# Hybrid encoder trunk: eight weight pieces of the second layer's gated MLP are cast, and their residuals formed, by transfers of GpSimd's queue

## The chip, the cores and the metric

The kernel runs on one core of one Trainium2 chip. The metric is the device time of one execution in microseconds (us). Before the change it is 857.34 us, the median of three runs (857.09 to 857.48).

The engines are TensorE (PE, matrix products; PEld is its loading of weights), VectorE (DVE), ScalarE (ACT), GpSimd (POOL) and SyncE (SP). SP issues nearly all transfers from DRAM. The matrix product reads its operands from on-chip memory and sums in PSUM.

## The reference

Two layers work on 256 tokens of width 1024. Each has a token mixer (pooling and dilated attention) and a gated MLP with a width-3 convolution. The change concerns the MLP's first product in the second layer:

```python
def _conv_ffn(xn, w_up, conv_w, conv_b, w_down):
    a, gval = jnp.split(xn @ w_up, 2, axis=-1)      # w_up: 1024 x 5632 (two halves of 2816)
    ...
    return (jax.nn.gelu(a) * gval) @ w_down

for layer in range(DEPTH):                          # DEPTH = 2
    h = h + _token_mixer(_rmsnorm(h, norm1[layer]), ...)
    h = h + _conv_ffn(_rmsnorm(h, norm2[layer]), w_up[layer], ...)
return _rmsnorm(h, norm_f)
```

All is float32. The weights are read once each, so the kernel streams them past 256 tokens.

## The kernel before

**Products in three passes.** The PE multiplies in the format float32r (fp32r in the profile). To keep float32 accuracy, each operand is split into a high part (the value cast to fp32r) and a low part (the value minus the high part). A product is then high x high + high x low + low x high, all summed in PSUM. For activations the parts lie in one tile (`x2`); for weights they are `wh` and `wl`.

**The class `Weights` (object `W`)** streams the weights. A *load* is a transfer of mostly 1 MB from DRAM into one of three `raw` buffers (`RAW`), issued by SP (L126). A *piece* is half a load, 128 x 1024 elements. Splitting a piece (`open_next`) is two instructions: ACT casts `raw` to `wh` (L191), then DVE subtracts `wh` from `raw` into `wl` (L192). There are five buffers for such pairs (`BUFS`). `get` hands the next piece to the products and first splits pieces ahead of it, in the MLP up to four ahead; `free` gives its buffers back after the products. So the cast of a piece waits until the PE has finished an older one.

**The order in the MLP.** `ORDER` lists the blocks: a0 g0, a1 g1, ... a4 g4, r5 are blocks of 512 columns of `w_up` (a and g are its two halves, r5 is the rest of both), and d0 to d4 are parts of `w_down`. A block has 1024 rows x 512 columns, that is four pieces of 256 rows; `by_rows` (L671) gets a piece, calls `v_sum` (L661) for both halves of the tokens, six products each, so twelve products of 128x512 a piece, and frees it. After a block DVE turns the sums by 32x32 blocks, SP moves the turned blocks between partitions (`up_turned<-up_rows`, 64 KB each, L691), and `two_up` (L1384) works out the convolution and the gate on ACT and DVE, alongside the products of later blocks.

The block a0 is begun inside the norm before it: `residual_mm` (L567) ends the mixer's output product, `Norm.add` (L456) adds up the squares of the new rows, POOL adds the parts (L467, L469) and takes the root (L472, `rstd`), DVE scales the rows (L485, `xn`), and the PE transposes them (L494, `xt_ps`). While this goes on for the second half of the tokens, the PE has 18 products of a0 on the first half to do (`begin_mlp`, L1318).

`keep_order` (L643) fixes the order of PE, ACT and DVE to that of the program text in this part. POOL and SP are ordered by the scheduler.

The tile `m2` (16 KB a partition) holds the merged branches of the mixer; its last readers are the output product's matmuls. In the second layer it is not used after that.

Of the kernel before, what the change touches and what calls it, by code (L numbers as in the profile page):

```python
# [10 lines left out]
F32 = mybir.dt.float32  # L11
F32R = mybir.dt.float32r
AF = mybir.ActivationFunctionType
ALU = mybir.AluOpType
AX = mybir.AxisListType

P = 128
D = 1024
# [8 lines left out]
DFF = 2816  # L27
# [10 lines left out]
PAIRS = (0, 1)  # L38
POOLED = {15: 0, 17: 1, 19: 2, 21: 3}
ORDER = "a0 g0 v0 a1 g1 a2 g2 a3 g3 a4 g4 r5 d0 d1 d2 d3 d4"  # L40
RING = 16
TWOS = (16, 20, 24, 28, 32, 36, 39, 43, 47, 51, 55)
VISITS = {
    "score": ((0, 1), (2, 3), (5, 6), (7, 8)), "expo": (3, 5, 8, 10), "norm": (4, 6, 9, 11),
    "turn": (5, 7, 10, 12), "parts": (13, 14, 19, 20), "weigh": (15, 16, 20, 21),
# [41 lines left out]
class Weights:  # L87
# [4 lines left out]


    RAW, BUFS, LOOK = 3, 5, 3

    def __init__(self, tc, pool, idle):
        self.tc, self.nc, self.pool, self.idle = tc, tc.nc, pool, idle
        self.loads, self.pieces = [], []
        self.n_loaded, self.n_split, self.n_got = 0, 0, 0
        self.raw, self.split = {}, {}  # L100
        self.live = set()
        self.behind, self.n_behind = (), 0
        self.n_scaled, self.gains = 0, None
        self.due = 0

    def add(self, src, shape, cuts, tag=None):

        n = len(self.loads)
        self.loads.append((src, shape, tag))
        return [(n, cut, c_shape) for cut, c_shape in cuts]  # L110

    def use(self, pieces, slots=()):
        slots = list(slots) + [None] * len(pieces)
# [35 lines left out]
    def _split(self, upto):  # L149
        nc = self.nc  # L150
        self.load(self.due)
        first = self.n_split
        while self.n_split < len(self.pieces):
            i = self.n_split
            n, cut, shape, slot = self.pieces[i]
            if i >= upto and (slot is None or i >= max(upto, first + 2) or i >= upto + 4 or i < 4):
                break
            if slot is None and len(self.live) == self.BUFS:
                break
            self.load(n + 1)  # L160
            with ExitStack() as queued:
                if i < self.n_behind:
                    for inst in self.behind:
                        queued.enter_context(self.tc.issue_after(inst.ins))
                for part in self.open_next():
                    for make in part:
                        make()
            self.due = n + self.RAW

    def open_next(self):  # L170

# [50 lines left out]
def encoder(ctx, tc, x, w_in, w_pool, pool_scale, w_a, w_b, w_o, norm1, norm2, w_up, conv_w,  # L222
# [11 lines left out]
    W = Weights(tc, wpool, big)  # L234
# [8 lines left out]
    def rows(w, r0, n=2, c0=0, width=1024, tag=None, pieces=2):  # L243

        src = w[r0 : r0 + n * P, c0 : c0 + width].rearrange("(k p) c -> p k c", p=P)
        h = n // pieces
        return W.add(
            src, (n, width), [((lambda t, j=j: t[:, j * h : (j + 1) * h, :]), (h, width)) for j in range(pieces)],
            tag,
        )  # L250

    for l in range(DEPTH):
        if l == 0:
            slots = (("m2", 0, 2), ("m2", 1, 2), ("ybig",), ("at2",))
            for j in range(2):
                kept = rows(w_in[l], j * 512, 4, C_V, 512)
                more = rows(w_in[l], j * 512, 4, C_V + 512, 512, "k1" if j else None)
                for n in range(2):
                    W.use(kept[n : n + 1], slots[2 * j + n : 2 * j + n + 1])
                    W.use(more[n : n + 1])  # L260
            W.n_scaled = len(W.pieces)
        else:
            W.use(rows(w_in[l], 512, 4, C_V, 512), (("ybig",), ("at2",)))
            for j in range(2):
                W.use(rows(w_in[l], j * 512, 4, C_V + 512, 512))

        def half_of(w, c0, half, n):
            for j in range(n):
                W.use(rows(w, j * 512, 4, c0 + half.start, 512))

        for half in HALVES:
            half_of(w_in[l], 0, half, 2)
        for c0 in (C_Q + 512, C_K + 512, C_Q + 1024, C_K + 1024):
            half_of(w_in[l], c0, HALVES[0], 2)
        for c in PAIRS:
            q = cols(w_in[l], C_Q + c * 256)
            k = cols(w_in[l], C_K + c * 256)
            if c == 0:
                pool = W.add(
                    w_pool[l].rearrange("g (k p) c -> p (g k) c", p=P), (8, 256),  # L280
                    [((lambda t, j=j: t[:, 4 * j : 4 * j + 4, :]), (4, 256)) for j in range(2)],
                )
                q.insert(1, pool[0])
                k.insert(1, pool[1])
            W.use(q + k)
        half_of(w_in[l], C_V + 1024, HALVES[0], 2)

        for half in HALVES:
            half_of(w_in[l], C_GP, half, 2)
        for half in HALVES:  # L290
            half_of(w_a[l], 0, half, 2)
            half_of(w_in[l], C_GA, half, 2)
            half_of(w_b[l], 0, half, 1)
        for c in range(4):
            W.use(rows(w_o[l], c * 256))
        slots = (("v1",), ("ybig",), ("at2",))
        for kind, n in ORDER.split():
            n = int(n)
            if kind == "v":
                if l + 1 < DEPTH:  # L300
                    W.use(rows(w_in[l + 1], 0, 4, C_V, 512), (("m2", 0, 2), ("m2", 1, 2)))
                continue
            for j in range(2):
                if kind == "d":
                    W.use(rows(w_down[l], (4 * n + 2 * j) * P))
                elif kind == "r":
                    src = w_up[l][j * 512 : (j + 1) * 512].rearrange("(k p) c -> p k c", p=P)
                    c0 = (4 * n * P, 4 * n * P + DFF)
                    W.use(
                        W.add(  # L310
                            tuple(src[:, :, c : c + 256] for c in c0), (4, 2, 256),
                            [
                                ((lambda t, j=j: t[:, 2 * j : 2 * j + 2].rearrange("p k h c -> p k (h c)")), (2, 512))
                                for j in (0, 1)
                            ],
                        )
                    )
                else:
                    p = rows(w_up[l], j * 512, 4, (kind == "g") * DFF + 4 * n * P, 512)
                    W.use(p, slots[2 * j : 2 * j + 2] if (kind, n) == ("a", 0) else ())  # L320
        W.use(rows(w_down[l], (NF - 2) * P))


    h = const.tile([P, 2, D], F32, name="h")
# [578 lines left out]
    for l in range(DEPTH):  # L903
# [296 lines left out]
        for c in PAIRS:  # L1200
            for n in range(4):
                src, rest = (halves(a) for a in proj(x2))
# [85 lines left out]
        m2 = []  # L1288
# [29 lines left out]
        def begin_mlp():  # L1318
# [12 lines left out]
            out=way[:, 0].rearrange("p j c r -> p c j r"),  # L1331
            in_=th[0][:, 1].rearrange("p (c j r) -> p c j r", c=4, j=4),
# [132 lines left out]
        for kind, n in ORDER.split():  # L1465
# [20 lines left out]
            n = int(n)  # L1486
# [39 lines left out]
```

## Time and profile before

| | |
|---|---|
| Device time, median of 3 runs | 857.34 us |
| Span of the profiled execution, first to last instruction | 856.1 us |
| Granted TensorE clock | 0.999 of full speed |
| POOL busy | 19.9 us, 53 instructions |
| DMA from DRAM | 160.65 MB read, 190 GB/s over the span |

The profile gives for its execution the span alone; the median of the timed runs lies 1.24 us above it, and what lies around the span (start and end of the program) is in that difference. The shares of busy time are means over stages; a stage is read from windows of the span. Matmuls are pipelined: one of 128x512 is shown as 0.39 us long, and the next starts before it ends, so a full PE is seen from the distance of the starts.

Two parts of the pipeline matter below. From about 669 us the PE does the second layer's a0; the blocks g0 to g4 run from 680.92 us. Twelve products make a piece. The pieces are numbered through the program: a0 has 230 to 233, g0 234 to 237, a1 238 to 241, and so on to g4 with 266 to 269.

### The profile page before, as it was taken

Reading aid. Unit: us, or ns where it says so; the run is one execution under the profiler, and the core shown is the slowest. Engines: PE = TensorE matmul, PEld = TensorE weight load, DVE = VectorE, ACT = ScalarE, POOL = GpSimd, SP = SyncE. Lnnn points to the kernel's source line nnn. Section 1 sums busy time; section 2 is a strip of 40 time slices with the busy share of each in tenths; the row PEclk is TensorE's granted clock in tenths of the full one; section 3 lists DMA queues with packets and bytes.
Section 4 is the critical chain, followed back from the end, with each engine's and each line's share of the span. In section 5 each row is a group of like instructions: output and inputs, shape, how many; then the busy total and the mean of one; then the engine's idle time right before and its main releaser. Section 6 shows DMA issues by size and latency. Waiting matters only on the chain.

```text
span 856.1 us, 11279 instructions
## 1 busy us (share of the span) xinstructions
PE 849.1 (99%) x4030; PEld 713.0 (83%) x4030; DVE 648.8 (76%) x918; ACT 476.9 (56%) x700; POOL 19.9 (2%) x53
## 2 busy tenths in 40 slices
PE   9999999999999999999999999999999999999997
PEld 7888888888888888888888889888888888888886
DVE  6967898566767788999656597986568658999874
ACT  7735475444545566767444445654445436766762
POOL 1120000000010000000000000000000000000001
PEclk9999999999999999999999999999999999999999
DMA  8787684764947777777626676758559376777751
GB/s 313 243 256 247 190 278 149 220 231 127 315 173 233 225 236 241 249 232 257 220 99 210 226 233 192 237 162 247 199 200 310 112 228 190 244 242 242 255 181 50
DMA packets 101340, 186.07 MB, mean 217 GB/s; under 512 B 9806, under 2 KB 28702, under 8 KB 101284
## 3 DMA queue, kind: packets, MB, share of 16 engines
q1 hardware_dynamic: 100484, 183.62, 64.9%
q0 software_dynamic: 496, 1.33, 0.5%
q8 instruction: 32, 0.52, 0.3%
q10 hardware_dynamic: 304, 0.40, 0.1%
q14 instruction: 24, 0.20, 0.1%
HBM read 160.65 MB, written 1.59 MB: 190 GB/s over the span
## 4 chain that ended last, share of the span: by engine, by line
PE 99%; POOLq 0%; DVE 0%; ACT 0%; issue 0%; DVEq 0%; POOL 0%; ACTq 0%
PE rows_ps L666 61%; PE res_ps L563 6%; PE res_ps L565 6%; PE res_ps L564 6%; PE v_ps L666 5%; PE proj_ps L535 3%; PE v_ps L788 3%; PE proj_ps L537 2%; PE s_ps L1076 1%; PE o_ps L1151 1%; PE s_ps L1071 1%; PE o_ps L1147 1%; PE xt_ps L494 1%; PE pool_ps L529 0%; PE pool_ps L527 0%; PE pool_ps L528 0%
## 5 line engine op out<-in xcount | busy, mean ns | idle before, releaser
L192 DVE TENSOR_TENSOR wl<-raw,wh 128x1024 fp32r<-128x1024 f32 x278 | 336.9, 1218 | 145.4 <-ACT wh L191 141.6
L666 PE MATMUL rows_ps<-wh,x 128*128 128x512 f32 x1344 | 420.1, 391 | 0.0
L191 ACT CAST wh<-raw 128x1024 fp32r<-128x1024 f32 x278 | 288.9, 1049 | 212.7 <-PE rows_ps L666 131.0
L666 PEld LDWEIGHTS rows_ps<-wh,x 128*128 128x128 f32 x1344 | 252.4, 188 | 52.2
L666 PE MATMUL rows_ps<-wl,x 128*128 128x512 f32 x672 | 261.6, 389 | 0.0
L666 PEld LDWEIGHTS rows_ps<-wl,x 128*128 128x128 f32 x672 | 126.2, 188 | 25.6
L563 PE MATMUL res_ps<-wh,actq 128*128 128x512 f32 (+1 forms) x152 | 57.5, 378 | 0.0
L564 PE MATMUL res_ps<-wl,actq 128*128 128x512 f32 (+1 forms) x152 | 57.4, 378 | 0.0
L565 PE MATMUL res_ps<-wh,actk 128*128 128x512 f32 (+1 forms) x152 | 57.4, 378 | 0.0
L666 PE MATMUL rows_ps<-wh,po 128*128 128x512 f32 x128 | 41.2, 393 | 0.0
L564 PEld LDWEIGHTS res_ps<-wl,actq 128*128 128x128 f32 x152 | 28.6, 188 | 5.4
L563 PEld LDWEIGHTS res_ps<-wh,actq 128*128 128x128 f32 x152 | 28.6, 188 | 5.4
L565 PEld LDWEIGHTS res_ps<-wh,actk 128*128 128x128 f32 x152 | 28.6, 188 | 5.3
L535 PE MATMUL proj_ps<-x,wh 128*128 128x512 f32 x128 | 32.2, 393 | 0.0
L701 DVE STREAM_TRANSPOSE up_rows<-rows_ps 128x512 f32<-128x512 f32 x40 | 26.3, 693 | 3.1 <-PE rows_ps L666 3.1
L666 PEld LDWEIGHTS rows_ps<-wh,po 128*128 128x128 f32 x128 | 24.0, 188 | 4.9
L1393 ACT ACTIVATE yg<-a,prm 128x256 f32<-128x256 f32 x44 | 26.5, 602 | 1.4
L563 PE MATMUL res_ps<-wh,m 128*128 128x512 f32 (+1 forms) x72 | 26.7, 371 | 0.0
L535 PEld LDWEIGHTS proj_ps<-x,wh 128*128 128x128 f32 x128 | 23.1, 189 | 4.2
L565 PE MATMUL res_ps<-wh,m 128*128 128x512 f32 (+1 forms) x72 | 26.4, 366 | 0.0
L564 PE MATMUL res_ps<-wl,m 128*128 128x512 f32 (+1 forms) x72 | 26.4, 366 | 0.0
L463 ACT ACTIVATE junk<-h 128x512 f32<-128x512 f32 (+1 forms) x19 | 10.5, 552 | 27.5 <-DVE h L461 27.5
(225 smaller groups left out, 1051.6 us busy)
## 6 DMA issues: line engine op xcount, KB each, us to landing
raw<-in_w_in_dram SPq DMA_DIRECT2D x56, 1024.0 KB, 5.5
raw<-in_w_up_dram SPq DMA_DIRECT2D x40, 1024.0 KB, 6.0
raw<-in_w_down_dram SPq DMA_DIRECT2D x22, 1024.0 KB, 5.8
up_turned<-up_rows SPq DMA_DIRECT2D x160, 64.0 KB, 3.9
raw<-in_w_a_dram SPq DMA_DIRECT2D x8, 1024.0 KB, 5.0
raw<-in_w_o_dram SPq DMA_DIRECT2D x8, 1024.0 KB, 5.1
qk<-qk_rows SPq DMA_DIRECT2D x64, 64.0 KB, 2.7
pt<-rows SPq DMA_DIRECT2D x64, 64.0 KB, 3.6
```

Source lines behind the costliest of these rows:

```text
L191: lambda: nc.scalar.copy(out=h, in_=src),
L192: lambda: nc.vector.tensor_sub(out=l, in0=src, in1=h.bitcast(F32)),
L463: nc.scalar.activation(junk, new, AF.Square, scale=D**-0.5, accum_out=ss[:, n : n + 1])
L535: nc.tensor.matmul(ps, wh(k), x2[:, k], start=(k == 0), stop=False)
L537: nc.tensor.matmul(ps[:, 1], wl(k), x2[:, k, 0], start=False, stop=(k == nk - 1))
L563: nc.tensor.matmul(ps, ah, wh, start=first, stop=False)
L564: nc.tensor.matmul(ps, ah, wl, start=False, stop=False)
L565: nc.tensor.matmul(ps, al, wh, start=False, stop=last)
L666: nc.tensor.matmul(ps, x2[:, 2 * n + j, part, t, :], w[:, j, :], start=(n + m == 0), stop=(n == of - 1 and m == 5),)
L701: nc.vector.transpose(out=out[:, :, t].rearrange("p j c r -> p c j r"), in_=ps[t].rearrange("p (c j r) -> p c j r", c=4, j=4),)
L788: return nc.tensor.matmul(ps[g][t], a[:, k, t, :], w[:, k % 2, :], start=k == 0 and kind == "hh", stop=k == KD - 1 and kind == "hl",)
L1393: nc.scalar.activation(y, aj, AF.Identity, bias=b, scale=w1)
```

## The change

In the second layer, in the blocks a1 to a4 and g1 to g4, the fourth piece (rows 768 to 1023 of the block: pieces 241, 245, 249, 253, 257, 261, 265, 269) no longer comes from a `raw` buffer. The load that held the third and the fourth piece is cut to the third (512 KB instead of 1 MB). The fourth goes another way, marked `DIRECT`:

- `fetch` (called four pieces ahead, `AHEAD`): a transfer on GpSimd's queue from DRAM into the high part `h`, which casts float32 to fp32r on the way.
- `take` (where the piece would have been split): ACT writes the negative of `h` into the low part `l`; a second transfer on GpSimd's queue reads the same 512 KB from DRAM again and adds them to `l`, which then holds the piece minus its high part.

The two parts lie in a ring of two pairs (`PAIRS`) in the tile `m2`. Such a piece uses neither `wh` nor `wl`, and is not counted among the five live ones.

```diff
+DIRECT = "direct"
 class Weights:
     RAW, BUFS, LOOK = 3, 5, 3
+    AHEAD, PAIRS = 4, 2
 ...
+    def direct(self, src, shape):
+        self.use([(src, None, shape)], [DIRECT])
 ...
             n, cut, shape, slot = self.pieces[i]
+            if slot == DIRECT and i >= upto:
+                break
 ...
             if slot is None and len(self.live) == self.BUFS:
                 break
+            self.fetch(i + self.AHEAD)
+            if slot == DIRECT:
+                self.take(i)
+                continue
             self.load(n + 1)
 ...
+    def fetch(self, upto):
+        while self.n_fetched < min(upto, len(self.pieces)):
+            i = self.n_fetched
+            self.n_fetched += 1
+            src, _, shape, slot = self.pieces[i]
+            if slot != DIRECT:
+                continue
+            if self.ring is None:
+                self.ring = self.idle.tile([P, self.PAIRS, 2, 1024], F32R, tag="m2", name="direct")
+            k, self.n_direct = self.n_direct % self.PAIRS, self.n_direct + 1
+            h, l = (
+                self.ring[:, k, part].rearrange("p (k c) -> p k c", c=shape[1]) for part in (0, 1)
+            )
+            self.split[i] = (h, l)
+            self.nc.gpsimd.dma_start(out=h, in_=src)
+
+    def take(self, i):
+        h, l = self.split[i]
+        self.n_split += 1
+        self.nc.scalar.mul(out=l, in_=h.bitcast(F32), mul=-1.0)
+        self.nc.gpsimd.dma_start(out=l, in_=self.pieces[i][0], accum_op=ALU.add)
 ...
             for j in range(2):
                 if kind == "d":
                     W.use(rows(w_down[l], (4 * n + 2 * j) * P))
+                elif kind in "ag" and l == 1 and j and n:
+                    c0 = (kind == "g") * DFF + 4 * n * P
+                    W.use(rows(w_up[l], 512, 2, c0, 512, pieces=1))
+                    W.direct(w_up[l][768:D, c0 : c0 + 512].rearrange("(k p) c -> p k c", p=P), (2, 512))
```

The lines of the changed kernel are shifted: its L198 is the casting transfer, L204 the negation, L205 the adding transfer; L228 is the cast that was L191, L707 the product that was L666, and L508, L510, L513 are the norm's three POOL instructions that were L467, L469, L472.

POOL's queue at the norm ahead of the second layer's MLP, before (`ss_5736` and `ss_5737` are the sums of squares of the two halves of the tokens, `rstd` their roots; the last two rows belong to the final norm):

```order
L472 TENSOR_TENSOR rstd_5882<-ss_5736,mhalf_77 128x1 [waits DVE_49,Pool_49]
L467 TENSOR_SCALAR ss_5737<-ss_5737 128x1 [waits Activation_49]
L469 TENSOR_TENSOR ss_5737<-ss_5737 128x1 [waits Activation_49,Pool_49] x2
L472 TENSOR_TENSOR rstd_5952<-ss_5737,mhalf_77 128x1 [waits DVE_49,Pool_49]
L467 TENSOR_SCALAR ss_7402<-ss_7402 128x1 [waits Activation_49]
L469 TENSOR_TENSOR ss_7402<-ss_7402 128x1 [waits Activation_49,Pool_49]
```

The same place in the changed kernel:

```order
L508 TENSOR_SCALAR ss_5737<-ss_5737 128x1 [waits Activation_49]
L510 TENSOR_TENSOR ss_5737<-ss_5737 128x1 [waits Activation_49,Pool_49]
L198 DMA direct_6060<-in_w_up_dram 128x2x512 [waits DMAHW3_49,DMAHW4_49,DMAHW2_49,DMAHW5_49,DMAHW1_49,DMAHW6_49,DMAHW0_49,DMAHW7_49,DVE_49,PE_49]
L510 TENSOR_TENSOR ss_5737<-ss_5737 128x1 [waits Activation_49,Pool_49]
L198 DMA direct_6060<-in_w_up_dram 128x2x512
L513 TENSOR_TENSOR rstd_5952<-ss_5737,mhalf_77 128x1 [waits Pool_49]
L205 DMA direct_6060<-in_w_up_dram 128x2x512 [waits Activation_49]
L205 DMA direct_6060<-in_w_up_dram 128x2x512 [waits DMASW3_49,Activation_49]
L198 DMA direct_6060<-in_w_up_dram 128x2x512 [waits DMASW4_49,DMASW0_49,PE_49]
L205 DMA direct_6060<-in_w_up_dram 128x2x512 [waits DMASW5_49,Activation_49]
```

The first two casting transfers (pieces 241 and 245) stand between the last additions of the norm and its root. The third (piece 249) stands behind the adding transfers of 241 and 245 and waits for the PE, which reads the ring's first pair for piece 241; from there casting and adding transfers alternate.

ACT's queue at the pieces 240 to 246, before (the number behind `wh` is the piece):

```order
L191 CAST wh240_6094<-raw120_6042 128x1024 [waits DMAHW6_49,DVE_49,PE_49]
L191 CAST wh241_6112<-raw120_6042 128x1024 [waits DVE_49,PE_49]
L191 CAST wh242_6132<-raw121_6076 128x1024 [waits DMAHW7_49,DVE_49,PE_49]
L191 CAST wh243_6154<-raw121_6076 128x1024 [waits DVE_49,PE_49]
L191 CAST wh244_6174<-raw122_6110 128x1024 [waits DMAHW0_49,DVE_49,PE_49]
L191 CAST wh245_6196<-raw122_6110 128x1024 [waits DVE_49,PE_49]
L191 CAST wh246_6222<-raw123_6152 128x1024 [waits DMAHW1_49,DVE_49,PE_49]
```

And in the changed kernel, from there to piece 249:

```order
L228 CAST wh240_6096<-raw120_6042 128x1024 [waits DMAHW6_49,DVE_49,PE_49]
L204 ACTIVATE direct_6060<-direct_6060 128x1024 [waits DMASW0_49]
L228 CAST wh242_6133<-raw121_6078 128x1024 [waits DMAHW7_49,DVE_49,PE_49]
L228 CAST wh243_6155<-raw121_6078 128x1024 [waits DVE_49,PE_49]
L228 CAST wh244_6175<-raw122_6112 128x1024 [waits DMAHW0_49,DVE_49,PE_49]
L204 ACTIVATE direct_6060<-direct_6060 128x1024 [waits DMASW1_49]
L228 CAST wh246_6222<-raw123_6153 128x1024 [waits DMAHW1_49,DVE_49,PE_49]
L228 CAST wh247_6240<-raw123_6153 128x1024 [waits DVE_49,PE_49]
L228 CAST wh248_6256<-raw124_6195 128x1024 [waits DMAHW6_49,DVE_49,PE_49]
L204 ACTIVATE direct_6060<-direct_6060 128x1024 [waits DMASW4_49,DMASW2_49]
```

The negation stands where the cast of that piece stood; it waits for the casting transfer, and no longer for the PE to free a buffer.

The PE at piece 241, before:

```order
L666 MATMUL rows_ps_6131<-wh240_6094,x2_5734 128x512
L666 MATMUL rows_ps_6130<-wh241_6112,x2_5734 128x512 [waits Activation_49]
L666 MATMUL rows_ps_6130<-wl241_6113,x2_5734 128x512 [waits DVE_49]
L666 MATMUL rows_ps_6130<-wh241_6112,x2_5734 128x512 x2
L666 MATMUL rows_ps_6130<-wl241_6113,x2_5734 128x512
```

And in the changed kernel:

```order
L707 MATMUL rows_ps_6131<-wh240_6096,x2_5734 128x512
L707 MATMUL rows_ps_6130<-direct_6060,x2_5734 128x512 [waits DMASW0_49]
L707 MATMUL rows_ps_6130<-direct_6060,x2_5734 128x512 [waits DMASW2_49]
L707 MATMUL rows_ps_6130<-direct_6060,x2_5734 128x512 x4
L707 MATMUL rows_ps_6131<-direct_6060,x2_5734 128x512 x6
```

The first product of the piece now waits for the casting transfer, the second for the adding one. The number of products is the same.

1 line of the change is left out of this document (added).

## The prediction

> **What bounds the kernel now.** I read the busy shares first, then the chain of work that ended last, then the PE's waits, then the stretch in which the changed pieces are used (692 to 780 us) and the last 10 us.
>
> ```profile
> span 856.1 us, 11279 instructions
> PE 849.1 (99%) x4030; PEld 713.0 (83%) x4030; DVE 648.8 (76%) x918; ACT 476.9 (56%) x700; POOL 19.9 (2%) x53
> PE 99%; POOLq 0%; DVE 0%; ACT 0%; issue 0%; DVEq 0%; POOL 0%; ACTq 0%
> PE gain_ps L377 <- DVE mhalf L366: 1.0, 1, 1.0
> 692.00:780.00 88.00, 88.00 (x390) 72.85 (x389) 72.81 (x105) 56.36 (x78) 0.00 (x0) 1.00 0.72 235
> 846.00:856.00 10.00, 4.12 (x25) 3.49 (x23) 4.36 (x11) 3.13 (x9) 1.92 (x6) 0.90 0.29 105
> ```
>
> The PE is the chain, 99% of it. The fourth row is the whole list of its waits: 1.0 us, at the start. In the stretch (columns: length, PE, PEld, DVE, ACT, POOL busy, clock, DMA share, GB/s) it is busy all 88 us, at full clock, while DVE has 15.2 us left, ACT 31.6 and the DMA engines 28%, or 24.6 us. Of the 7.0 us in which the PE is idle at all, 5.9 lie in the last 10 us, in the final norm and the store, which the change doesn't touch.
>
> A pipelined PE can look full and yet be slowed between its starts, so I look at the starts. The PE's first product of piece 234, and the casts that wait for the PE to free a buffer:
>
> ```profile
> 680.92 0.39 PE L666 MATMUL rows_ps<-wh,x 128*128 128x512 f32 x1
> 681.12 1.06 ACT L191 CAST wh<-raw 128x1024 fp32r<-128x1024 f32 x1 [1.09 <-PE v_ps L666]
> 683.84 1.05 ACT L191 CAST wh<-raw 128x1024 fp32r<-128x1024 f32 x1 [1.66 <-PE rows_ps L666]
> 711.04 1.05 ACT L191 CAST wh<-raw 128x1024 fp32r<-128x1024 f32 x1 [1.67 <-PE rows_ps L666]
> 716.48 1.05 ACT L191 CAST wh<-raw 128x1024 fp32r<-128x1024 f32 x1 [0.57 <-PE rows_ps L666]
> 749.12 1.05 ACT L191 CAST wh<-raw 128x1024 fp32r<-128x1024 f32 x1 [0.57 <-PE rows_ps L666]
> ```
>
> From 681.12 to 683.84 is one piece, 2.72 us, or 0.227 us a product. From 681.12 to 749.12 are 68.00 us, exactly 25 pieces. The PE doesn't lose a tenth of a microsecond there. **It can't gain from a lighter ACT or DVE; the change can only leave it alone or make it wait.** Piece p starts at 680.92 + 2.72 (p - 234): piece 241 at 699.96, 249 at 721.72.
>
> **The change, part by part.**
>
> *Removed: eight subtractions on DVE. Exchanged: eight casts on ACT.*
>
> ```profile
> L192 DVE TENSOR_TENSOR wl<-raw,wh 128x1024 fp32r<-128x1024 f32 x278 | 336.9, 1218 | 145.4 <-ACT wh L191 141.6
> L191 ACT CAST wh<-raw 128x1024 fp32r<-128x1024 f32 x278 | 288.9, 1049 | 212.7 <-PE rows_ps L666 131.0
> 715.28 0.63 ACT L1406 ACTIVATE y<-yg 128x512 f32<-128x512 f32 x1 [0.33 <-DVE yg L1397]
> ```
>
> DVE loses 8 x 1.218 = 9.7 us, all of it beside a full PE: 0 us. A negation of 1024 elements lies between the cast's 1.05 us and twice the 0.63 us of an ACTIVATE of 512; I take 1.1. That is under 1.7 us more on ACT, inside its 31.6 idle: 0 us.
>
> *Added: sixteen transfers issued by POOL.* The nearest rows are POOL's own transfers at the start:
>
> ```profile
> L435 POOL DMA_DIRECT2D fd<-fsb x3: 518/540/746, 40.0 to 43.3; - x3
> L438 POOL DMA_DIRECT2D bt<-fd x5: 747/749/805, 44.3 to 48.1; - x5
> DMA to landing us min/median/max: 5.1/5.7/6.7
> ```
>
> An issue holds POOL 0.52 to 0.81 us; I take 0.75. The third row belongs to `bt<-fd` (256 KB each). Fourteen of the issues meet a POOL that has nothing else to do: 0 us. Two stand ahead of the norm's root, behind which the PE's transposes wait:
>
> ```profile
> 668.51 0.28 PE L565 MATMUL res_ps<-wh,m 128*128 128x256 f32 x1
> 669.02 0.19 POOL L469 TENSOR_TENSOR ss<-ss 128x1 f32<-128x1 f32 x1 [0.72 <-ACT junk L463]
> 670.40 0.19 POOL L469 TENSOR_TENSOR ss<-ss 128x1 f32<-128x1 f32 x1 [1.19 <-ACT junk L463]
> 670.68 0.57 POOL L472 TENSOR_TENSOR rstd<-ss,mhalf 128x1 f32<-128x1 f32 x1
> 671.28 1.67 DVE L485 SCALAR_TENSOR_TENSOR xn<-h,rstd,gain 128x256 f32<-128x256 f32 x4 [0.70 <-POOL rstd L472]
> 673.19 0.60 PE L494 MATMUL xt_ps<-ident,xn 128*128 128x128 f32 x4
> ```
>
> The first casting transfer waits for the last reader of `m2` (668.79) and stands behind the addition of 669.02: it runs from 669.25 to 670.0, in a gap of POOL that lasts to 670.40. The second comes behind the addition of 670.40 and moves the root from 670.68 to about 671.4, and `xn` from 671.28 to 672.0. The transposes of 673.19 need half of `xn`, 0.84 us, so 672.85. What hides the 0.75 us is the 18 products of a0 ahead of the transposes; 0.35 us of that cover are left: 0 us. If an issue lasts 2 us (an estimate at over twice the 0.81), the root is late by 2.7 us and the PE waits 1.6.
>
> *Moved: when a direct piece is ready.* Three things must follow each other inside the ring's cycle: the casting transfer of piece p starts when the PE has left piece p - 8; ACT negates; the adding transfer lands by the second product of p. From the end of p - 8 to there are 7 x 2.72 + 0.23 = 19.3 us. Landings of the weights' loads in the stretch (the third row is of all loads into `raw` from 692 to 792), and below them all loads of the kernel:
>
> ```profile
> raw<-in_w_up_dram SPq DMA_DIRECT2D x11, 1024.0 KB, 6.3
> raw<-in_w_up_dram SPq DMA_DIRECT2D x4, 512.0 KB, 5.3
> DMA to landing us min/median/max: 5.2/5.3/7.4
> DMA to landing us min/median/max: 3.9/5.6/8.6
> ```
>
> With 5.7 us (POOL's landing) for each transfer the chain is 5.7 + 1.1 + 0.4 for two hand-overs + 5.7 = 12.9 us: 6.4 to spare. The tighter bound is ACT's order. Piece 249 was cast at 711.04; its negation stands there. The casting transfer, issued at about 702.9 behind the products of 241, lands at 708.6 and even at 7.4 us by 710.3, so it makes ACT no later. If the negation starts at 711.04, the adding transfer goes out at 712.3 and has until 721.95: **9.65 us**. (It may start earlier, up to the landing, because direct pieces leave buffers free; then up to 12 us.) The trace shows no transfer that adds. From below it is 5.3 us, as the plain load; from above twice 8.6, if it reads its destination as long as its source, 17.2. I take 7.5: POOL's 5.7 and some 1.8 for the second reading, by the rate below. That is inside 9.65, so 0 us, with 2 us of cover.
>
> The Trainium skill ("DMA: Bandwidth & Descriptors", section "Anatomy of one DMA") has about 2.0 us plus the bytes at 436 GB/s for a transfer of this queue, an estimate of 3.2 us for 512 KB. The trace disagrees: a plain 512 KB takes 5.3 beside the other loads.
>
> *More for the DMA engines.* Their time for a piece, from the stretch (36 to 60 us) where both queues work; columns are packets, MB, share of 16 engines:
>
> ```profile
> q1 hardware_dynamic: 3252, 6.24, 75.4%
> q0 software_dynamic: 496, 1.33, 19.6%
> ```
>
> SP's queue moved 6.24 MB in 0.754 x 24 = 18.1 us (345 GB/s), POOL's 1.33 MB in 4.7 us (283 GB/s). A piece of 0.524 MB is 1.52 or 1.85 us of all engines. Eight casting transfers cost 8 x 0.33 = 2.6 us more than the loads they replace; eight adding ones 14.8, or 29.6 if they read their destination as long again. The sum, 17.4 or 32.2 us, stands against 24.6 idle. I take 17.4: it fits.
>
> **Sum:** 856.1 + 0 = 856.1 us of span, so the median of 857.34 stays; I say 857.4.
>
> **Rivals.**
>
> *A. The adding transfer lands late, and the PE waits for it.* For it: a second read of the source, on a queue whose landings are no faster than SP's, and a limit of 9.65 us that is only 1.7 times 5.7. Against: the negation may come up to 2.3 us earlier. It decides from a landing of about 10 us on. At 11.4 (twice 5.7) each late piece costs 1.75 us. Late are at least pieces 249, 257 and 265 (a wait at one pushes the next away, but the ring starts again from it), at most all eight: 5 to 14 us, 863 to 871. At 17.2 it would be 23 us and more.
>
> *B. The DMA engines fill up.* At 32.2 us against 24.6 idle the stretch grows by up to 7.6 us: 865. For it: in parts of the stretch they are as good as full already, since 0.72 is a mean. Against: the loads of `raw` shrink by 8 x 0.5 MB, and stand five pieces ahead. The Trainium skill (same page, "Issuing engines are not separate DMA queues") says that transfers run on the same 16 engines whoever issues them, so that another issuing engine saves only issue time: by that rule the 4 MB that are read twice come on top. No run here shows yet whether the trace agrees.
>
> *C. The norm waits for POOL.* If casting issues take 2 us: +1.6 us, 859.0, still within what counts as no change.
>
> *D. The change doesn't relieve what ends last, but a wait that the trace can't see:* a lighter DVE makes an unseen loss go. Against: 25 pieces without a loss. At most the 1.1 us of PE idle time outside the last 10 us go: 856.2, which is no change by the bound below; for more the shown starts would have to be wrong.
>
> **How the numbers follow.** A measurement of this kernel can tell about 0.2% from no change, that is 1.7 us. No change: 0.66. A: 0.17, B: 0.09, both slower by over 1.7 us. C: 0.04, a quarter of it over the bound. D: 0.04, of which I give 0.03 to a gain over the bound, for starts that are wrong. So faster 0.03, same 0.70 (0.66, 0.03 of C, 0.01 of D), slower 0.27 (A, B, 0.01 of C). The range reaches from 856.1, just under D's 856.2, to 868, the middle of A and above B; beyond lie some 0.08 of A above and 0.03 below. The likeliest case alone is 857.0 to 858.0.
>
> **What would show it.** Right: the PE full from 692 to 780, its products in the stretch 0.227 us apart, no wait of L707 for `direct`; DVE's busy time some 9.7 us less; adding transfers that land in under 9.6 us; a DMA share in the stretch of about 0.9. A shows as waits of L707 for a DMA into `direct`, every second or every direct piece; B as casts (L228) that wait for `raw` longer than before and as a DMA share of 1; C as a PE that waits for `xn` at about 673. Wrong would be the whole if the PE showed another distance of starts.

## The result

The changed kernel takes **863.23 us** (median of 3 runs, 862.09 to 865.63) against 857.34 before: 1.0072 times as long, 95% interval 1.0049 to 1.0094. It is slower by 0.7%, inside the range, but the likeliest case, no change, was wrong. The profiled execution is the run of 865.63 us; its span is 7.8 us longer than that of before.

The profile after, in the order in which before was read: busy shares and chain from the page, then the PE's waits for the weights and the norm (us in total, times, longest), then the stretch from 692 to 780 us.

```profile
span 863.9 us, 11304 instructions
PE 851.3 (99%) x4030; PEld 714.0 (83%) x4030; DVE 641.1 (74%) x910; ACT 478.7 (55%) x700; POOL 35.6 (4%) x69
PE 91%; DMA 4%; issue 2%; ACT 1%; POOL 1%; DVE 0%; SPq 0%; POOLq 0%; DVEq 0%; ACTq 0%
PE rows_ps L707 <- DMA direct<-in_w_up_dram: 4.2, 2, 2.5
PE xt_ps L535 <- DVE xn L526: 1.3, 1, 1.3
692.00:780.00 88.00, 86.14 (x379) 70.69 (x377) 61.43 (x90) 51.16 (x71) 12.89 (x13) 1.00 0.95 258
```

The PE is no longer the whole chain: DMA has 4% of it. The PE's idle time rose from 856.1 - 849.1 = 7.0 us to 863.9 - 851.3 = 12.6, by 5.6, and the two new rows of waits hold 4.2 + 1.3 = 5.5 of that. The other 2.2 us of the 7.8 are busy time (851.3 against 849.1) with the same 4030 products. The PE's timeline at the last two direct pieces (265 and 269), and its clock there (the columns are those of the stretch above, the clock is the last but two), say where:

```profile
766.56 0.39 PE L707 MATMUL rows_ps<-direct,x 128*128 128x512 f32 x1
768.66 2.81 PE L707 MATMUL rows_ps<-direct,x 128*128 128x512 f32 x11 [1.71 <-DMA direct<-in_w_up_dram]
...
779.46 0.39 PE L707 MATMUL rows_ps<-direct,x 128*128 128x512 f32 x1
782.35 4.36 PE L707 MATMUL rows_ps<-direct,x 128*128 128x512 f32 x11 [2.50 <-DMA direct<-in_w_up_dram]
783.00:787.00 4.00, 4.00 (x13) 3.16 (x12) 3.38 (x6) 3.77 (x6) 0.00 (x0) 0.66 0.89 365
787.00:791.00 4.00, 4.00 (x19) 3.31 (x18) 3.97 (x8) 1.86 (x3) 0.00 (x0) 1.00 0.82 276
```

Each time the first product of the piece runs (the cast is there) and the second waits: the adding transfer is late, by 1.71 and by 2.50 us. After the longer wait the granted clock was 0.66, and eleven products took 4.36 us instead of 2.81. These 1.55 us are most of the 2.2.

Why are the adding transfers late? POOL's timeline from piece 257 on; L205 is an adding transfer, L198 a casting one, the number in brackets is how long POOL stood idle before it:

```profile
737.35 1.19 POOL L205 DMA_DIRECT2D direct<-in_w_up_dram  x1 [10.38 <-ACT a L1433]
738.09 1.21 POOL L198 DMA_DIRECT2D direct<-in_w_up_dram  x1
748.55 1.21 POOL L205 DMA_DIRECT2D direct<-in_w_up_dram  x1 [9.25 <-ACT a L1433]
749.29 1.23 POOL L198 DMA_DIRECT2D direct<-in_w_up_dram  x1
760.21 1.19 POOL L205 DMA_DIRECT2D direct<-in_w_up_dram  x1 [9.70 <-ACT a L1433]
760.95 1.21 POOL L198 DMA_DIRECT2D direct<-in_w_up_dram  x1
772.92 1.20 POOL L205 DMA_DIRECT2D direct<-in_w_up_dram  x1 [10.76 <-ACT a L1433]
```

The casting transfers wait for nothing of their own: each runs 0.74 us behind the adding transfer that stands ahead of it in POOL's queue. The adding transfer waits for its negation, which waits for its casting transfer to land, which was issued behind the adding transfer before. That is a loop, and its period reads off the L205 rows: 748.55 - 737.35 = 11.20 us, then 11.66 and 12.71. The PE needs a direct piece every four pieces, 4 x 2.72 = 10.88 us. Each turn falls behind, and the lead of the adding transfer over the PE's first product of its piece shrinks: from piece 249 on it is 10.5, 9.7, 7.5, 7.1, 6.4 and 6.5 us (the last is 779.46 - 772.92, behind the wait of 1.71). The first two steps, down to 7.5, are not the queue's: the casting transfers of 249, 253 and 257 still waited for the PE and went out at 704.47, 715.35 and 726.23, 10.88 us apart, but they landed after 6.6, 7.4 and 9.7 us. The landings of casting transfers (first row) and adding ones (second), what the two DMA queues took of the engines' time from 692 to 780 us, and from the page SP's 512 KB loads (median us to landing):

```profile
DMA to landing us min/median/max: 3.9/8.3/10.5
DMA to landing us min/median/max: 6.5/7.9/9.4
q1 hardware_dynamic: 9808, 15.47, 56.4%
q0 software_dynamic: 3691, 7.13, 38.7%
raw<-in_w_up_dram SPq DMA_DIRECT2D x16, 512.0 KB, 7.6
```

The casts land 8.3 us behind their issue, up to 10.5; the DMA engines are taken for 95.1% of the stretch, where it was 72%. The casts that take longest to land are those that stand closest behind an adding transfer of their own queue: 6.6 us at 6.1 us behind it, 7.4 at 2.9, 9.7 at 2.0, and 9.1, 9.5 and 10.5 at 0.74.

And the norm, in POOL's and the PE's timeline:

```profile
668.67 0.19 POOL L510 TENSOR_TENSOR ss<-ss 128x1 f32<-128x1 f32 x1 [0.72 <-ACT junk L504]
671.37 0.77 POOL L198 DMA_DIRECT2D direct<-in_w_up_dram  x1 [2.50 <-issue]
672.16 0.21 POOL L510 TENSOR_TENSOR ss<-ss 128x1 f32<-128x1 f32 x1
672.30 0.75 POOL L198 DMA_DIRECT2D direct<-in_w_up_dram  x1
673.07 0.58 POOL L513 TENSOR_TENSOR rstd<-ss,mhalf 128x1 f32<-128x1 f32 x1
674.32 0.74 PE L535 MATMUL xt_ps<-ident,xn 128*128 128x128 f32 x4 [1.32 <-DVE xn L526]
```

The first casting transfer holds the queue until 672.14, the root runs at 673.07 instead of 670.68, and the PE waits 1.32 us for `xn`.

### The profile page after: what moved, and what is told of

The parts are those of the page before. It is cut to its first block, busy times and chain, and to the rows that moved or that the text cites. A ratio compares the mean times of both kernels' runs of the same rounds, so it can differ in the third digit from the quotient of the medians.

```text
span 863.9 us, 11304 instructions
## 1 busy us (share of the span) xinstructions
PE 851.3 (99%) x4030; PEld 714.0 (83%) x4030; DVE 641.1 (74%) x910; ACT 478.7 (55%) x700; POOL 35.6 (4%) x69
## 4 chain that ended last, share of the span: by engine, by line
PE 91%; DMA 4%; issue 2%; ACT 1%; POOL 1%; DVE 0%; SPq 0%; POOLq 0%; DVEq 0%; ACTq 0%
PE rows_ps L707 55%; PE res_ps L604 6%; PE res_ps L605 6%; PE res_ps L606 6%; PE v_ps L707 5%; PE proj_ps L576 3%; DMA direct<-in_w_up_dram 3%; PE v_ps L829 3%; PE proj_ps L578 2%; PE s_ps L1117 1%; PE o_ps L1192 1%; DMA up_turned<-up_rows 1%; PE s_ps L1112 1%; PE o_ps L1188 1%; PE xt_ps L535 1%
## 5 line engine op out<-in xcount | busy, mean ns | idle before, releaser
L229 DVE TENSOR_TENSOR wl<-raw,wh 128x1024 fp32r<-128x1024 f32 x270 | 326.9, 1217 | 137.3 <-ACT wh L228 133.2
L707 PE MATMUL rows_ps<-wh,x 128*128 128x512 f32 x1280 | 401.5, 391 | 0.0
L228 ACT CAST wh<-raw 128x1024 fp32r<-128x1024 f32 x270 | 280.7, 1049 | 207.1 <-PE rows_ps L707 118.8
L707 PEld LDWEIGHTS rows_ps<-wh,x 128*128 128x128 f32 x1280 | 240.4, 188 | 49.7
L707 PE MATMUL rows_ps<-wl,x 128*128 128x512 f32 x640 | 249.1, 389 | 0.0
L707 PEld LDWEIGHTS rows_ps<-wl,x 128*128 128x128 f32 x640 | 120.2, 188 | 24.4
L707 PE MATMUL rows_ps<-wh,po 128*128 128x512 f32 x128 | 41.2, 393 | 0.0
L1435 DVE SCALAR_TENSOR_TENSOR yg<-a,prm,yg 128x255 f32<-128x255 f32 x44 | 21.1, 481 | 19.2 <-ACT yg L1434 19.2
L508 POOL TENSOR_SCALAR ss<-ss 128x1 f32<-128x1 f32 x8 | 1.8, 221 | 680.9 <-ACT junk L504 680.9
L707 PE MATMUL rows_ps<-direct,x 128*128 128x512 f32 x96 | 25.2, 411 | 4.2 <-DMA direct<-in_w_up_dram 4.2
L707 PEld LDWEIGHTS rows_ps<-wh,po 128*128 128x128 f32 x128 | 24.0, 188 | 4.9
L604 PE MATMUL res_ps<-wh,m 128*128 128x512 f32 (+1 forms) x72 | 26.7, 371 | 0.0
```

Of the source, the lines that this page charges most:

```text
L228: lambda: nc.scalar.copy(out=h, in_=src),
L229: lambda: nc.vector.tensor_sub(out=l, in0=src, in1=h.bitcast(F32)),
L604: nc.tensor.matmul(ps, ah, wh, start=first, stop=False)
L707: nc.tensor.matmul(ps, x2[:, 2 * n + j, part, t, :], w[:, j, :], start=(n + m == 0), stop=(n == of - 1 and m == 5),)
L1435: nc.vector.scalar_tensor_tensor(out=y[:, 1:], in0=aj[:, : S - 1], scalar=w0, in1=y[:, 1:], op0=ALU.mult, op1=ALU.add)
```

## The experiments

Three theories, which can all hold: **N**, the norm waits because casting transfers stand ahead of its root; **S**, the loop on POOL's in-order queue is longer than the PE's 10.88 us; **L**, the DMA engines are nearly full, and that alone makes transfers late. The kernel before, run beside these, had medians of 857.56 to 857.79 us.

| kernel | median us | lowest to highest, runs | ratio to before, 95% |
|---|---|---|---|
| the change again | 862.63 | 861.23 to 867.66, 6 | 1.0045 to 1.0090 |
| root first | 861.41 | 860.58 to 863.47, 5 | 1.0027 to 1.0053 |
| three pairs | 859.24 | 857.85 to 861.60, 11 | 1.0012 to 1.0030 |
| both | 860.76 | 857.80 to 863.82, 9 | 1.0023 to 1.0050 |
| light adding | 859.39 | 859.01 to 859.73, 11 | 1.0008 to 1.0026 |
| four pieces | 859.35 | 859.15 to 862.22, 11 | 1.0013 to 1.0030 |
| both, light adding | 857.72 | 857.28 to 858.61, 11 | 0.9990 to 1.0007 |
| four pieces, root first | 858.18 | 857.06 to 860.04, 11 | 0.9998 to 1.0016 |
| both, POOL negates | 860.94 | 857.73 to 863.56, 11 | 1.0017 to 1.0044 |

**The change again**, with nothing edited:

> The changed kernel itself, measured again as the baseline of the other runs. Expected 862 to 863 us (863.23 before, 862.09 to 865.63), with PE waits of about 1.3 us for xn at the norm and of about 4 us in all for the adding transfers of the last direct pieces.

862.63 us, with the same two waits for `direct` (1.65 and 2.52 us) and the same 1.3 us for `xn`. Here the clock stayed at full speed behind the wait of 2.52 us.

**Root first.** The casting transfers may be issued only behind the norm's root:

```diff
-            self.nc.gpsimd.dma_start(out=h, in_=src)
+            with self.tc.issue_after(self.root.ins):
+                self.nc.gpsimd.dma_start(out=h, in_=src)
 ...
-                nc.gpsimd.tensor_tensor(out=r, in0=ss[:, 3:4], in1=mhalf, op=ALU.pow)
+                W.root = nc.gpsimd.tensor_tensor(out=r, in0=ss[:, 3:4], in1=mhalf, op=ALU.pow)
```

> The casting transfers are held back until the norm's root has been taken, nothing else changes. Theory N (the first two casting transfers delay the root on POOL, and that costs the PE its 1.3 us wait for xn): the wait for xn goes, the time is 1.3 us under the changed kernel, about 861.5. Rival (the PE would have waited for something else there, or the first casting transfers now come too late): no gain, or a new wait at piece 241. Both leave the waits for the adding transfers of pieces 265 and 269.

861.41 us, 1.2 us less than the change. POOL's rows: the root stands right behind the last addition, and the transfers behind it.

```profile
671.22 0.19 POOL L511 TENSOR_TENSOR ss<-ss 128x1 f32<-128x1 f32 x1 [1.19 <-ACT junk L505]
671.49 0.57 POOL L514 TENSOR_TENSOR rstd<-ss,mhalf 128x1 f32<-128x1 f32 x1
672.75 1.50 POOL L199 DMA_DIRECT2D direct<-in_w_up_dram  x2 [0.69 <-DVE xn L527]
```

The PE's wait for `xn` is gone, the waits for `direct` (2.3 us) are not. N holds by the profile; the 1.2 us between the medians agree with the wait of 1.3, though the two intervals overlap.

**Three pairs.** A third pair for the ring (in the room of `bt`, which is no longer needed then), and the ring is filled eight pieces ahead instead of four:

```diff
-    AHEAD, PAIRS = 4, 2
+    AHEAD, PAIRS = 8, 3
 ...
-                self.ring = self.idle.tile([P, self.PAIRS, 2, 1024], F32R, tag="m2", name="direct")
+                ring = self.idle.tile([P, 2, 2, 1024], F32R, tag="m2", name="direct")
+                third = self.idle.tile([P, 2, 1024], F32R, tag="bt", name="third")
+                self.ring = ring[:, 0], ring[:, 1], third
 ...
-                self.ring[:, k, part].rearrange("p (k c) -> p k c", c=shape[1]) for part in (0, 1)
+                self.ring[k][:, part].rearrange("p (k c) -> p k c", c=shape[1]) for part in (0, 1)
 ...
-    bt = const.tile([P, HPG, NT * P], F32, name="bt")
+    bt = big.tile([P, HPG, NT * P], F32, tag="bt", name="bt")
```

> A third pair in the ring and casting transfers fetched two direct pieces ahead, so that on POOL's queue each casting transfer stands behind the adding transfer of the piece two before it and no longer of the piece just before. Bytes and transfers are the same. Theory S (a loop on POOL's queue: adding transfer n, casting transfer n+1, its landing of 8 to 10 us, negation, adding transfer n+1, is longer than the PE's 10.9 us for a block, so each piece is later than the last): the lead of the adding transfers stays at 9 us or more and the PE does not wait for them; left is the norm's 1.3 us, so about 858.8. Theory L (the DMA engines are full, the adding transfers land late whatever the order): the landings stay at 8 to 10 us, the PE still waits 3 to 5 us, about 862.

859.24 us, 3.4 less than the change, and 0.2 us are left of the waits for `direct`. The wait for `xn` is gone from this profile too, although casting transfers still stand ahead of the norm's root, so the 3.4 us are not those of the loop alone. (Of the 1.9 us by which this execution is still longer than before, 1.4 lie ahead of the norm: a0's first product starts at 670.40 instead of 668.99.) A casting transfer now goes out one turn earlier. POOL's rows, and ACT's cast ahead of the negation of piece 265:

```profile
732.98 1.19 POOL L207 DMA_DIRECT2D direct<-in_w_up_dram  x1 [5.91 <-ACT direct L206]
737.20 0.74 POOL L200 DMA_DIRECT2D direct<-in_w_up_dram  x1 [3.03 <-PE rows_ps L709]
744.04 1.21 POOL L207 DMA_DIRECT2D third<-in_w_up_dram  x1 [6.10 <-ACT a L1435]
755.21 1.05 ACT L230 CAST wh<-raw 128x1024 fp32r<-128x1024 f32 x1 [4.30 <-DMA raw<-in_w_up_dram]
758.03 1.19 POOL L207 DMA_DIRECT2D direct<-in_w_up_dram  x1 [9.21 <-ACT direct L206]
```

The casting transfer (L200) is 4.2 us behind the adding one and waits for the PE's products, and the period is 744.04 - 732.98 = 11.06 us instead of 11.2 to 12.7. The next one is 13.99 us, but not by the loop: the casting transfer of that piece, 265, had gone out at 737.20 and landed 8.3 us later; its negation stood on ACT behind a cast that waited 4.30 us for an ordinary load. S holds in so far as the waits went when the loop was loosened. The edit loosens two things, the order on the queue and the time that a landing may take (one turn more), and doesn't tell them apart.

**Both** edits together:

> Both: three pairs, and casting transfers behind the norm's root. Theories N and S together: no wait of the PE is left, 857.3 us as before the change. Theory L: still 860 to 861.

860.76 us at the median, from 857.80 to 863.82. The profile was of the run of 857.80: no wait of the PE for `direct` or `xn` at all, with DMA engines that are entirely full in the stretch (share 1.00).

```profile
692.00:780.00 88.00, 88.00 (x390) 72.90 (x389) 66.12 (x98) 54.45 (x78) 12.11 (x12) 1.00 1.00 276
```

By N and S alone every run should have looked like this one. So something is left that comes and goes, and L is the candidate. (That three pairs alone have the lower median is within this spread: the two intervals overlap, and their profile had no wait for `xn` left to take away.)

**Light adding.** The change, with adding transfers that bring 16 of each 512 columns; most of the residual of the eight pieces is left out:

```diff
-        self.nc.gpsimd.dma_start(out=l, in_=self.pieces[i][0], accum_op=ALU.add)
+        self.nc.gpsimd.dma_start(out=l[:, :, 0:16], in_=self.pieces[i][0][:, :, 0:16], accum_op=ALU.add)
```

> The adding transfers bring only 16 of each 512 columns (most of the residual of the eight pieces is left out); the order of GpSimd's queue, the two pairs and the norm's wait stay as they are in the changed kernel. If the loop on the queue is long because the DMA engines are nearly full, the casting transfers land in about 6.5 us instead of 8.3 at the median, the loop (landing, negation 1.06, 0.3, issues 0.75 and 1.2 at most) falls to about 9.5 us, below TensorE's 10.88 us a block, TensorE's waits of 4.2 us for these transfers go, and only the norm's 1.3 us is left: about 858.7 us (858.3 to 859.2). If the order of the queue alone makes the waits, whatever the landings are, some 3 us of them stay: 861 or more.

859.39 us, 0.2 us above the expected band, and with 0.7 us between the lowest and the highest run. POOL's rows, the landings of the casting transfers, and the stretch:

```profile
743.51 1.21 POOL L205 DMA_DIRECT2D direct<-in_w_up_dram  x1 [5.87 <-ACT a L1433]
747.78 0.74 POOL L198 DMA_DIRECT2D direct<-in_w_up_dram  x1 [3.06 <-PE rows_ps L707]
754.59 1.19 POOL L205 DMA_DIRECT2D direct<-in_w_up_dram  x1 [6.07 <-ACT a L1433]
DMA to landing us min/median/max: 4.1/4.6/5.5
692.00:780.00 88.00, 88.00 (x390) 72.93 (x389) 68.36 (x101) 55.91 (x79) 12.85 (x13) 1.00 0.80 239
```

Two pairs, the same queue in the same order, but the casts land in 4.6 us instead of 8.3: the casting transfer waits for the PE again, the period is 754.59 - 743.51 = 11.08 us, the PE is full, and only `xn` is waited for (1.6 us). (The light adding transfers also land sooner themselves, in 4.0 us at the median instead of 7.9, so that a shorter lead would do.) So the order on the queue does harm only with the long landings, and these come with the bytes of the adding transfers. S and L are two halves of one cause. Whether these bytes count because they fill the DMA engines or because they stand on the casts' own queue isn't separated: with three pairs, at a DMA share of 0.98 but 4.0 to 4.6 us behind the adding transfer, the casts landed in 4.8 to 8.6 us.

**Both, light adding.** The two edits and the light transfers (most of the residual of the eight pieces is left out):

> Three pairs, the root first, and adding transfers of 16 of each 512 columns (most of the residual of the eight pieces is left out). The same without the light transfers had 860.8 us at the median, spread from 857.8 to 863.8, and its fastest run showed no wait of TensorE. If that spread is made by the DMA engines being full in the stretch (chance waits and what follows them), it is gone here: 857.4 to 858.2 us with no more spread than the kernel before. If it comes from something else that these pieces bring (the third pair, the fetching ahead), the spread and some 2 us stay.

857.72 us, no different from before, and the spread is gone. The difference to light adding alone is 1.7 us, near the wait of 1.6 for `xn` there. What was left with both edits goes with the bytes of the adding transfers: 860.76 against 857.72.

**Four pieces.** Only the `g` blocks keep a direct piece:

```diff
-                elif kind in "ag" and l == 1 and j and n:
+                elif kind == "g" and l == 1 and j and n:
```

> Only the four pieces of the g blocks come directly, one in 21.8 us of TensorE; the a blocks are split by the engines as before the change. By the theory of the queue's loop (11.2 to 12.7 us a piece) the loop has 9 us to spare, no wait for a transfer is left, and the kernel is at the time before plus the norm's wait of 1.3 us: about 858.7 us (858.3 to 859.3). By the theory that a nearly full set of DMA engines itself costs TensorE time, half of the 20.7 us of additional traffic gives half of the loss: about 860.2 us.

859.35 us, just above the first theory's band and under the 860.2 of the other. No wait for `direct`; the casts land in 4.0 to 4.4 us, and the PE waits 1.6 us for `xn` and 0.8 for an ordinary piece.

**Four pieces, root first**, both edits as shown:

> Four direct pieces and the casting transfers held until the norm's root. By the theory that the loss is made of the queue's loop, the norm's wait and the full DMA engines, nothing of any is left: 857.3 to 857.9 us, no different from the kernel before, since TensorE was the bound there and has the same products. If direct pieces cost TensorE in some other way, 859 or more.

858.18 us, 0.3 above the expected band, its interval reaches 1: no different from before by the bound of 0.2%. It does the whole computation, and it is the best such version that ran; none beats the kernel before, since the PE's products are the same.

**Both, looked at twice more**, for two executions of different length:

> The kernel with three pairs and the root first once more, for a profile of an execution near its median of 860.8 us (the profile taken before was of its fastest, 857.8, and showed no wait of TensorE). If the spread of 857.8 to 863.8 us is made by the nearly full DMA engines, a slower execution shows TensorE waiting for raw's or direct's DMA between 690 and 790 us, 1 to 3 us in all, with or without a lower granted clock behind it. If it shows no such wait and the clock is granted in full, the spread lies elsewhere.

> The same kernel as the run before it, for a second profile: expectation as there. Two profiles of different times tell which stretch makes the difference.

The first run took 863.50 us (span 861.7), the second 858.36 (span 856.6). In each the only wait for `direct` is at piece 265. POOL's issue of its adding transfer, the PE's row, and the clock behind it, of the first run:

```profile
756.65 1.19 POOL L208 DMA_DIRECT2D direct<-in_w_up_dram  x1 [9.94 <-ACT a L1436]
768.09 5.06 PE L710 MATMUL rows_ps<-direct,x 128*128 128x512 f32 x11 [3.16 <-DMA direct<-in_w_up_dram]
770.00:775.00 5.00, 5.00 (x15) 3.94 (x14) 2.53 (x4) 0.95 (x2) 0.00 (x0) 0.59 1.02 275
```

and of the second:

```profile
757.01 1.19 POOL L208 DMA_DIRECT2D direct<-in_w_up_dram  x1 [10.07 <-ACT direct L207]
765.79 2.79 PE L710 MATMUL rows_ps<-direct,x 128*128 128x512 f32 x11 [0.63 <-DMA direct<-in_w_up_dram]
```

The transfer was issued at the same place and landed 768.09 - 756.65 = 11.4 us later in the first run, 8.8 in the second. The wait is 2.5 us longer, and the eleven products behind it took 5.06 us instead of 2.79 at a clock of 0.59: 4.8 of the 5.1 us between the two spans. Between these two executions the difference is one late landing, enlarged by the clock. In both the lead was already short: 764.54 - 756.65 = 7.9 and 764.77 - 757.01 = 7.8 us to the piece's first product, against 765.14 - 754.28 = 10.9 in the run of 857.80. That the other slow executions are of this kind isn't shown.

**Both, POOL negates.** In both runs that adding transfer had been issued behind a negation on ACT that stood behind a cast of an ordinary piece, which had waited about 5 us. So the negation was taken off ACT:

```diff
-        self.nc.scalar.mul(out=l, in_=h.bitcast(F32), mul=-1.0)
+        self.nc.gpsimd.tensor_scalar_mul(l, h.bitcast(F32), -1.0)
```

> Three pairs and the root first, and GpSimd instead of ScalarE negates the eight casts, so that a negation stands behind no cast of ScalarE that waits for raw. With ScalarE the adding transfer of piece 265 was issued at 756.65 and 757.01 us, behind a cast that had waited about 5 us for a load or for room, against 753.04 with light transfers; it landed 11.4 or 8.8 us later, and TensorE waited 3.2 or 0.6 us. If ScalarE's order is the step by which full DMA engines reach TensorE, the adding transfers are issued 3 us or more earlier, no wait for direct is left, and the spread goes: 857.3 to 858.3 us. If a late landing alone is enough, 860 to 861 us at the median stay, with waits for direct. GpSimd's negation of 128x1024 elements should take 1 to 3 us; were it 5 or more, the queue is a new loop and the time is 860 or more.

860.94 us, and the spread as before, as if ACT's order weren't the step that decides. But the test isn't clean. POOL's rows, and the longest of the PE's waits for weights:

```profile
740.87 1.24 POOL L208 DMA_DIRECT2D third<-in_w_up_dram  x1 [0.30 <-POOL third L207]
741.64 1.24 POOL L201 DMA_DIRECT2D direct<-in_w_up_dram  x1
751.42 3.16 POOL L207 TENSOR_SCALAR direct<-direct 128x1024 fp32r<-128x1024 f32 x1 [8.54 <-DMA direct<-in_w_up_dram]
754.88 1.22 POOL L208 DMA_DIRECT2D direct<-in_w_up_dram  x1 [0.30 <-POOL direct L207]
PE res_ps L608 <- DVE wl L232: 1.1, 2, 0.8
```

A negation takes 2.8 to 3.8 us there, and the loop is back, at 754.88 - 740.87 = 14.0 us, with casting transfers 0.77 us behind adding ones. The PE now waits mostly for ordinary pieces (the last row is the longest; 1.9 us in all between 802 and 811 us, behind the last direct piece), and 0.5 us for `direct`. Why these ordinary pieces come late was not followed. So this run doesn't rule out ACT's order, and whether late direct landings or late loads weigh more in the spread stays open.

## Why the prediction was wrong

The time lies inside the range, at the price of rival A; the case held likeliest, no change, failed.

*The bound* was right: the PE can't gain. DVE has 278 - 270 = 8 subtractions less, 7.7 us less busy time in all, and that brought nothing. The negation takes 1.06 us (1.1 taken), a casting issue 0.74 to 0.77 alone (0.75 taken); an adding one takes 1.2.

*The step that failed is the cover of 9.65 us: ACT's order as "the tighter bound", with the casting transfer "issued at about 702.9" behind the products of its ring slot.* It was right for the piece for which it was worked out: the casting transfer of 249 went out at 704.47 and its adding transfer at 712.50, where 712.3 was predicted. I carried it over to the later pieces as if every turn began anew. One turn of the PE further each time, the adding transfers of 253, 257, 261, 265 and 269 should have been issued at 723.2, 734.1, 744.9, 755.8 and 766.7; they were at 724.23, 737.35, 748.55, 760.21 and 772.92, late by 1.0, 3.3, 3.6, 4.4 and 6.2 us (the PE itself was 1.3 us late there, and 3.3 at 269). Two things made this. The casting transfers of 253 and 257 went out behind the PE's products, as worked out, and it was their landings of 7.4 and 9.7 us that came late. From 261 on the queue is added: 738.09, 749.29 and 760.95 are 1.0, 1.3 and 2.1 us behind the spacing of 10.88. By an estimate from these rows, with the same landings but without the queue's part, the last two waits would have been 0.4 us each instead of 1.71 and 2.50. The list of POOL's queue shown ahead of the prediction has casting and adding transfers alternate, but I asked only when the ring frees a slot, not what stands ahead of the transfer on its own queue. Three pairs took the waits away, and gave each landing one turn more as well. The ring's own chain, which had "6.4 to spare" of 19.3 us, had nothing left either: with what piece 265 measured it is 9.5 + 1.1 + 0.4 + 8.4 = 19.4 us.

*The term that made the loop long was mis-sized:* the landing of a casting transfer. 5.7 us were taken, from POOL's transfers of 256 KB, half as large, with 7.4 (the longest of the loads into `raw` in the stretch) as the worst; it took 8.3 at the median. Light adding, with 4.6, has no wait for `direct` left in the same order. The adding landing, on which rival A was hung, was sized well: 7.5 taken, 7.9 measured. So A came by another way than its point of decision (a landing of about 10 us): not the landing grew, its cover of 9.65 us shrank, to 6.6 and 6.8 for the last two pieces, whose adding transfers took 8.4 and 9.4 us. Only these two of the eight were late, where A had at least 249, 257 and 265. That the time met A's lower end, 863, is partly luck: the profiled execution has 4.2 us of A's waits, and the norm's 1.3 and the clock's 1.6, which A's sum doesn't hold, beside them.

*The DMA engines:* 17.4 us more were taken. The share rose from 72.1% to 95.1% of 88 us, so 20.2 us; POOL's queue moved 7.13 MB in 0.387 x 88 = 34.1 us, 209 GB/s where 283 was taken. "It fits" was true of the mean and said nothing of landings. B's sign, casts that wait longer for `raw`, hardly came: from 692 to 792 us ACT waited 7.8 us for `raw` against 7.5 before, and both edits ran one execution at a share of 1.00 without a wait of the PE. The share alone doesn't set the landings either: the casts took 4.2 us at the median at 0.81 (four pieces), 6.6 at 0.83 (four pieces, root first), 7.4 at 1.00 (both) and 8.3 at 0.95 (the change). The Trainium skill's rule ("DMA: Bandwidth & Descriptors", section "Issuing engines are not separate DMA queues"), that transfers share the same 16 engines whoever issues them, is borne out here: with the full adding transfers on POOL's queue SP's sixteen 512 KB loads landed in 7.6 us at the median, with light ones in 6.2.

*The norm:* C's mechanism came, at 1.3 us for its 1.6, but not by an issue of 2 us. The step that failed is "it runs from 669.25 to 670.0": it ran from 671.37 (the last section has what stands in between). The cover of 0.35 us was far too thin to rest on. Root first, the two kernels with four pieces (859.35 to 858.18) and the two with light adding (859.39 to 857.72, where the third pair differs too) give 1.2 to 1.7 us for this step.

## What to carry to other kernels

When a transfer is put on a queue whose instructions run in order, ask of every transfer what stands ahead of it on that queue and what that waits for; if the wait leads back to the transfer before, write down the loop's period and hold it against the period of the bound, over all turns and not for one. A landing time read from smaller transfers, or beside less traffic, is a lower end where the DMA engines are at 95%; a spare buffer in the loop made its size matter far less. And an engine that is full pays for what is put ahead of its rare small helpers: the norm's root had 0.35 us of cover, and two issues ate it, the first of which started 2.1 us later than was taken.

## What the runs showed of the hardware

After a wait of 2.04 us (root first), 2.50 (the change) and 3.16 (both, the first look), the PE's clock fell, to 0.67, 0.66 and 0.59 over the 4 to 5 us behind it, and eleven products took 3.96, 4.36 and 5.06 us instead of 2.79. After 1.65, 1.71 and, in the change run again, 2.52 us it did not. So a wait of 2 to 3 us can cost half as much again or more, or not. The Trainium skill ("TensorE: Matmul & The Clock Gate", section "Part 1: The HAM clock gate (the "warmup" mystery)") puts the fall behind an idle window of about 3.4 us, with free-running windows; these traces show it behind shorter waits. That nearly equal ones differ would fit free-running windows, but no run here shows them.

The first casting transfer of the change started at 671.37, though all that the other engines had ahead of it was done by 670.23 (the end of DVE's last instruction before it). The page calls the idle time "issue". POOL stood idle there for 2.5 to 2.8 us in all four profiles with two pairs and the transfers ahead of the root, and for 0.4 to 0.7 us where the transfers stood behind the root or a third pair was there. At least 1.1 us of it have no instruction as owner. The DMA view has one packet of 8 KB there, of the kind `instruction` (in the change at 669.69; the row is of 669.5 to 670 us):

```profile
q14 instruction: 1, 0.01, 6.2%
```

In all nine profiles that put this wait down to "issue" the first casting transfer starts 1.7 us behind that packet. With three pairs alone the packet moved at 666.9, ahead of this place, and the idle time was 0.65 us. So POOL seems to wait there for its next instructions. That the packet is POOL's isn't shown; it comes 1.0 to 1.3 us behind an addition of the norm on POOL each time.

A negation of 128x1024 takes 1.05 us on ACT and 2.8 to 3.8 on POOL.
